# Ring tiles of split weights 64 bytes longer, and half the scratch for dynamic transfers

## The chip, the cores and the metric

The kernel runs on one NeuronCore of a Trainium2 chip. The metric is the device time of one execution in microseconds. A kernel is run several times and the median is taken; one more execution is recorded by the hardware profiler, and the profile and the trace are of that one.

The engines are named as in the profile: PE (matmuls), PEld (PE's weight loads, which overlap matmuls), DVE (VectorE), ACT (ScalarE), POOL (GpSimd), SP (SyncE, which issues most of the transfers).

## The reference

One layer of a hybrid encoder block in float32, 512 tokens by 1024 features: a norm, one input projection, three kinds of attention over its columns (4 + 6 + 6 heads), an output projection into the residual, a gated MLP with a causal convolution of width 3, and a gated embedding at the end.

```python
hn = rms_norm(h, ln_mix)
z = hn @ w_in                                  # 1024 x 3590, split into heads
o = concatenate([o_a, o_b, o_c])               # three kinds of softmax attention
h = h + o @ w_out                              # 1024 x 1024
u = rms_norm(h, ln_ffn) @ w_up                 # 1024 x 5632
c = conv_b + sum(conv_w[j] * shifted(u, 2 - j) for j in range(3))
h = h + (silu(c[:, :2816]) * c[:, 2816:]) @ w_down   # 2816 x 1024
gate = sigmoid(rms_norm(h, ln_ple) @ w_ple_gate)
h = h + (p @ w_ple_proj) * gate
```

## The kernel before

**Split operands.** Every float32 operand of a large matmul is split into a rounded part (float32r, "hi") and the rest ("lo"). ACT writes hi as a cast, DVE writes lo as raw - hi (in a few places POOL does, or an adding transfer). A product is then three matmuls, hi x hi, hi x lo and lo x hi, which `mm3` (line 223) issues into one PSUM bank. Its first operand is the stationary one (128 x 128), its second the moving one (up to 512 columns).

**Rings of weight tiles.** The pool `pi` (line 148) holds three rings: `wraw` with 4 tiles, `whi` and `wlo` with 8 each, all [128, 768] in 4-byte elements, that is 3072 bytes in each partition. Three places take tiles from them: `load_w` (line 151) for the input projection and the output projection, `first_products` (line 312) for the weights A0 of the first products, and `in_turn` (line 193) for the MLP and the gate, which keeps tiles and hands them out in turn: 7 of `whi`, 7 of `wlo`, and 6 raw ones, of which four are `wraw`, the fifth is the last of `whi` and the sixth the last of `wlo`. In the profile the ring tiles are named w_raw, w_hi, w_lo, and A_h, B_h, C_l, wo_h and so on.

**What is stationary.** In the input projection (`project`, line 442) a slice of Th or Tl, the split activations, is stationary, and 256 to 384 columns of a weight tile move (A_z, A0b_z, A1b_z, B_z, C_z). In the output projection (wo), the up projection (u, sX, sY, sZ), the down projection (dn_X, dn_Y, dn_Z) and the gate (pg, pp), a 128-column slice of a weight tile is stationary. What moves there is 512 columns of Th or Tl, or 256 columns of the tiles xh, xl, g_ah and g_al.

**Where the tiles lie.** The scratch of the transfers that POOL issues lies at byte 0 of each partition and is 16384 bytes long. Behind it come constants, then h, Th, Tl, some small tiles, and the rings. The pools of the attention (p1) and of the MLP (mp) are counted from the other end of the partition and share that room one after the other. In the program's memory map the places, as bytes modulo 512, are:

| tiles | place modulo 512 |
|---|---|
| h, Th, Tl, all tiles of the three rings | 128 |
| MLP: xh, xl, g_ah, g_al, c, hn, su, sm, pp (pool mp) | 128 |
| attention: oall, q, k, kl, bias | 192 |
| attention: V, zn, ptc | 352 |
| attention: pth, ptl, ot | 480 |

A slice of 128 elements is 512 bytes, so every slice of a ring tile lies at the same place as its tile. The rings end at byte 128640, and mp begins at that byte.

**Order of work.** The attention half (up to some 300 us) is ordered by the framework's scheduler, which simulates the engines from the instructions and their shapes. Behind it, a planner in the kernel (from line 1007) puts tasks in order by costs and due times that are written as functions of the element counts; DVE, ACT, POOL and SP then follow that order exactly. SP issues the loads of raw tiles; such a load waits until the split that read the tile before is done. POOL issues the adding transfers which form sums of weight blocks in DRAM (dsum, usum; `add_sums`, line 1168), one at a time. These go through queue 0, and so do the adding transfers of `load_w` (line 174).

Of the kernel before, what the change touches and what calls it, by code (L numbers as in the profile page):

```python
# [8 lines left out]
F32 = mybir.dt.float32  # L9
F32R = mybir.dt.float32r  # L10
# [5 lines left out]
P = 128  # L16
# [62 lines left out]
def kernel(ctx: ExitStack, tc: tile.TileContext, x, xt0, xt, pt_in, small, bias_c,  # L79
# [9 lines left out]
    nc = tc.nc  # L89
    def f32(ap):  # L90
        return ap.bitcast(F32)
# [52 lines left out]
    def col(c0, i=0):  # L144
        return cols[:, c0 + i : c0 + i + 1]


    pi = ctx.enter_context(tc.tile_pool(name="pi", bufs=1))
    W = {"pool": pi, "n": 768, "raw": 4, "hi": 8, "lo": 8}

    def load_w(src_fn, nk, m, n, name, eng=dve, gain=None, later=False):

        wp, we = W["pool"], W["n"]
        raw = wp.tile([P, we], F32, tag="wraw", bufs=W["raw"], name=f"{name}_r")
        for dst, src in src_fn(raw):
            dma = sp.dma_start(out=dst, in_=src)
            if later:
                tc.keep_in_program_order(dma)
        hi = wp.tile([P, we], F32R, tag="whi", bufs=W["hi"], name=f"{name}_h")
        lo = wp.tile([P, we], F32R, tag="wlo", bufs=W["lo"], name=f"{name}_l")  # L160
        hv, lv = (t[:, : nk * n].rearrange("p (k c) -> p k c", k=nk) for t in (hi, lo))
        rv = raw[:, : nk * m].rearrange("p (k c) -> p k c", k=nk)
        if later:
            def split():
                act.copy(hv[:, :, :m], rv)
                eng.tensor_tensor(out=lv[:, :, :m], in0=rv, in1=f32(hv[:, :, :m]), op=ALU.subtract)
                return hv, lv

            return split
        if eng == "dma":  # L170

            act.copy(hv[:, :, :m], rv)
            act.activation(lv[:, :, :m], rv, AF.Copy, scale=-1.0)
            nc.gpsimd.dma_start(out=lv[:, :, :m], in_=rv, accum_op=ALU.add)
            return hv, lv
        if gain is not None and eng is nc.gpsimd:
            for k in range(nk):
                eng.tensor_scalar(rv[:, k], rv[:, k], gain[:, k : k + 1], 1.0, ALU.mult, ALU.mult)
        if gain is None or eng is nc.gpsimd:
            act.copy(hv[:, :, :m], rv)  # L180
            eng.tensor_tensor(out=lv[:, :, :m], in0=rv, in1=f32(hv[:, :, :m]), op=ALU.subtract)
        else:
            for k in range(nk):
                hk, lk, rk = (v[:, k, :m] for v in (hv, lv, rv))
                act.activation(hk, rk, AF.Copy, scale=gain[:, k : k + 1])
                dve.scalar_tensor_tensor(lk, rk, gain[:, k : k + 1], f32(hk), ALU.mult, ALU.subtract)
        return hv, lv
# [5 lines left out]
    def in_turn(what, n):  # L193
        ring = RING[what]
        if len(ring) < n:
            tag = what
            if what == "raw" and len(ring) >= W["raw"]:
                tag = ("hi", "lo")[(len(ring) - W["raw"]) % 2]
            ring.append(pi.tile([P, 768], F32 if what == "raw" else F32R, tag=f"w{tag}", bufs=W[tag], name=f"w_{what}{len(ring)}"))
        else:  # L200
            ring.append(ring[-n])
        return ring[-1]

    def raw_tile():
        return in_turn("raw", NRAW)

    def split(t, n, gain=None, to=None, eng=dve):

        hi, lo = to or [in_turn(q, NHI)[:, :n] for q in ("hi", "lo")]
        if gain is None:  # L210
            act.copy(hi, t[:, :n])
            eng.tensor_tensor(out=lo, in0=t[:, :n], in1=f32(hi), op=ALU.subtract)
        else:
            act.activation(hi, t[:, :n], AF.Copy, scale=gain)
            dve.scalar_tensor_tensor(lo, t[:, :n], gain, f32(hi), ALU.mult, ALU.subtract)
        return hi, lo
# [21 lines left out]
    def tcol(T, k, t):  # L238
        return T[k // 4][:, k % 4, t * P : (t + 1) * P]
# [28 lines left out]
    def load_x(t):  # L268
        tc.keep_in_program_order(nc.sync.dma_start(out=h[:, t, :], in_=x[t * P : (t + 1) * P, :]))
# [36 lines left out]
    def stats(t):  # L306
        token_stats(t, h[:, t, :], ap.tile([P, D], BF16, tag="e3", bufs=2, name=f"n1_sq{t}"))
        done("n", t)
# [3 lines left out]
    def first_products():  # L312
        for k in range(KD):
            n = 384
            if k % 2 == 0:
                wh, wl = (pi.tile([P, 768], F32R, tag=f"w{q}", bufs=W[q], name=f"A0_{k // 2}_{q}") for q in ("hi", "lo"))
            a = slice((k % 2) * n, (k % 2 + 1) * n)
            th, tl = Th[k // 4][:, k % 4, :], Tl[k // 4][:, k % 4, :]
            g = h[:, 3, 0:1] if k == 0 else col(C_MIX, k)
            if k == 0:  # L320
                for c in (slice(0, H), slice(H, S)):
                    dve.tensor_scalar(th[:, c], XB[k][:, c], g, 1.0, ALU.mult, ALU.mult)
            elif k == 3:
                dve.tensor_scalar(th, XB[k], g, 1.0, ALU.mult, ALU.mult)
            else:
                act.activation(th, XB[k], AF.Copy, scale=g)
            act.copy(wh[:, a], WA[k])
            dve.tensor_tensor(out=wl[:, a], in0=WA[k], in1=f32(wh[:, a]), op=ALU.subtract)
            dve.scalar_tensor_tensor(tl, XB[k], g, f32(th), ALU.mult, ALU.subtract)
            for i, (ta, w) in enumerate(((Th, wh), (Th, wl), (Tl, wh))):  # L330
                for t in range(NT):
                    pe.matmul(z0[t][:, :n], tcol(ta, k, t), w[:, a], start=k == 0 and i == 0, stop=k == KD - 1 and i == 2)
            if k == 1:
                load_x(3)
        ws = [w() for w in first_b]
        for t in range(NT):
            stats(t)
        ev = [in_unit("A0", 0, 384, t, None, []) for t in range(NT)]

        rs = [ev[t][0](rest=False) for t in range(2)]  # L340
        for t in range(NT):
            ev[t][1](rs[t])
            if t < 2:
                rs.append(ev[t + 2][0](rest=False))
        for t in range(NT):
            ev[t][0](sums=False)
        return ws
# [105 lines left out]
    def in_unit(pr, part, n, t, ws, prefetch):  # L453

        name = f"{pr}{'b' if part else ''}"
        if t == 0:
            ZN[pr, part] = ap.tile([P, NT, 2 * P], F32, tag="zn", bufs=2, name=f"{name}_zn")
            if part == 0:
                V[pr] = ap.tile([P, NT, 2 * P], F32R, tag="V", bufs=3, name=f"{pr}_V")
        if pr == "A0" and part == 0:  # L460
            z = z0[t]
        else:
            z = bank("tots"[t] if pr == "A0" else "z", f"{name}_z{t}")

        def evac(sums=True, rest=True):
            if not rest:
                return qk_sums(z, t, name)
            if part == 0:
                v = V[pr]
                vh = bass.AP(v.tensor, v[:, t, :].offset, [v.ap[0], [192, 2], [1, HD]])  # L470
                zv = z[:, 2 * P : 3 * P].rearrange("p (g c) -> p g c", c=HD)
                act.activation(vh, zv, AF.Copy, scale=rstd[:, t, 2:3])
                dve.scalar_tensor_tensor(v[:, t, HD : HD + P].rearrange("p (g c) -> p g c", c=HD), zv,
                                               rstd[:, t, 2:3], f32(vh), ALU.mult, ALU.subtract)
            elif n > 2 * P:
                dve.scalar_tensor_tensor(fg[:, t, 0:6], z[:, 2 * P : 2 * P + 6], rstd[:, t, 2:3], fgb,
                                               ALU.mult, ALU.add)
            return qk_sums(z, t, name) if sums else None

        def evac_done(rs=None):  # L480
            qk_scale(z, ZN[pr, part], t, rs or evac())
            done("in", pr, part, t)

        if pr == "A0" and part == 0:
            return evac, evac_done
        return project(ws, n, t, z, evac_done, prefetch)
# [369 lines left out]
    for j, (pr, part, *_) in enumerate(PARTS[1:], 1):  # L856
        n = w_in[j].shape[3]
        nxt = []
        if j + 1 < len(PARTS):
            q = PARTS[j + 1]  # L860
# [109 lines left out]
    for f in SEVEN:  # L970
        w = bass.AP(cols.tensor, cols[:, C_CONV0 + NF + f : C_CONV0 + NF + f + 1].offset, [cols.ap[0], [2 * NF, 3]])
# [694 lines left out]
    while ready:  # L1666
        q = ready.pop()
# [27 lines left out]
    while order:  # L1695
# [3 lines left out]
        if now:  # L1699
            q = now[0]  # L1700
        else:
            tr = [(trial(q)[0], q) for q in can]
            first_at = max(min(x for x, _ in tr), clock["dve"])
            q = min((q for x, q in tr if x <= first_at + 0.1), key=lambda q: q.dl)

            late = min((q for x, q in tr if x <= first_at + SLACK), key=lambda q: q.dl)
            q = late if late.dl < q.dl - URGENT else q
# [74 lines left out]
```

## Time and profile before

| | us |
|---|---|
| median of 3 runs | 712.01 (711.25 to 712.97) |
| profiled execution, its time | 713.37 |
| profiled execution, span from the first to the last instruction | 711.5 |
| PE busy | 695.4 |
| DVE busy | 545.8 |
| ACT busy | 394.2 |
| POOL busy | 223.1 |

The rows of the profile that the prediction quotes are of these kinds. A row of the window view has the stretch, its length, the busy time and count of PE, PEld, DVE, ACT and POOL, the granted share of PE's clock, the busy share of the DMA engines and GB/s. A row of the waits has who waited for whom, total us, times, longest. A row of the timeline has start, length, engine, operation, tiles, shape and count. A row of the groups has line, engine, operation, output<-inputs (for matmuls: moving and stationary in no fixed order), shapes and count, then busy us, mean ns of one, and the idle time in front. All of them stand at line 105, which is the helper that issues each operation. Numbers in tile names are left out, so u stands for u0 to u43.

### The profile page before, as it was taken

To read this page: it belongs to the slowest core of one execution; us is meant where nothing else is said; L and a number is where in the kernel's file an instruction comes from. 1 tells how busy PE (TensorE), PEld (TensorE's weight loads), DVE (VectorE), ACT (ScalarE), POOL (GpSimd) and SP (SyncE) were. 2 spreads that over 40 slices of the span, in tenths; PEclk is the share of its full clock that TensorE was granted. 3 is DMA by queue.
4 is the path that set the end of the run, shared out by engine and by line. 5 is a ranking of instruction groups with operands and counts; after the bars stand their busy time and mean duration, and the time that the engine had idled before them with its cause. 6 is when DMAs were issued, how large, how long until landed. Compare 5 with 4: busy or idle time off the path is not lost.

```text
span 711.5 us, 11539 instructions
## 1 busy us (share of the span) xinstructions
PE 695.4 (98%) x4028; PEld 622.6 (88%) x4028; DVE 545.8 (77%) x1110; ACT 394.2 (55%) x737; POOL 223.1 (31%) x324
## 2 busy tenths in 40 slices
PE   9999999999999999999999999999999999999997
PEld 8988889988999988868888899988988888999786
DVE  7668887887878874788887884798776787788764
ACT  6746766766666762566454542554444555546831
POOL 4576776767665440420011110111101110001310
PEclk9999999999999999999999999999999999999999
DMA  9454669646335313452786888867986683652531
GB/s 329 174 150 101 195 178 241 210 158 197 105 122 179 126 42 115 142 195 95 171 178 136 244 194 187 194 165 197 230 206 141 145 210 82 216 164 82 177 111 67
DMA packets 48472, 116.52 MB, mean 164 GB/s; under 512 B 5495, under 2 KB 7159, under 8 KB 48413
## 3 DMA queue, kind: packets, MB, share of 16 engines
q1 hardware_dynamic: 40476, 96.59, 41.9%
q0 software_dynamic: 7648, 18.88, 16.7%
q8 instruction: 32, 0.52, 0.3%
q10 hardware_dynamic: 288, 0.30, 0.1%
q14 instruction: 28, 0.22, 0.1%
HBM read 108.53 MB, written 31.47 MB: 197 GB/s over the span
## 4 chain that ended last, share of the span: by engine, by line
PE 78%; DVE 7%; DMA 6%; ACT 4%; POOL 2%; issue 2%; SPq 0%; ACTq 0%; DVEq 0%; POOLq 0%
PE u L105 30%; PE dn_X L105 9%; PE C_z L105 6%; PE pg L105 6%; PE wo L105 5%; PE dn_Y L105 4%; PE B_z L105 4%; PE dn_Z L105 2%; DMA bias_B<-fk_d 1%; PE sX L105 1%; DMA h<-in_x_dram 1%; DMA waq<-in_w_in_dram 1%; PE C_s L105 1%; PE C_po L105 1%; PE A_z L105 1%
## 5 line engine op out<-in xcount | busy, mean ns | idle before, releaser
L105 PE MATMUL u<-Tl,w_hi 128*128 128x512 f32 x320 | 125.0, 391 | 0.5 <-DVE Tl L105 0.5
L105 PE MATMUL u<-Th,w_hi 128*128 128x512 f32 x320 | 124.8, 390 | 0.0
L105 PE MATMUL u<-Th,w_lo 128*128 128x512 f32 x320 | 124.6, 389 | 0.0
L105 ACT CAST w_hi<-w_raw 128x768 fp32r<-128x768 f32 (+1 forms) x116 | 88.2, 783 | 64.1 <-PE dn_X L105 21.1
L105 DVE TENSOR_TENSOR w_lo<-w_raw,w_hi 128x768 fp32r<-128x768 f32 (+1 forms) x114 | 101.5, 909 | 18.2 <-ACT w_hi L105 17.2
L105 DVE SCALAR_TENSOR_TENSOR c<-u,cols,c 128x511 f32<-128x511 f32 x80 | 59.5, 746 | 22.3 <-ACT c L105 21.3
L105 PEld LDWEIGHTS u<-Tl,w_hi 128*128 128x128 f32 x320 | 60.1, 188 | 13.5 <-DVE Tl L105 1.3
L105 PEld LDWEIGHTS u<-Th,w_hi 128*128 128x128 f32 x320 | 60.1, 188 | 12.6 <-ACT Th L105 0.5
L105 PEld LDWEIGHTS u<-Th,w_lo 128*128 128x128 f32 x320 | 60.1, 188 | 12.6 <-POOL w_lo L105 0.2
L105 ACT ACTIVATE c<-u,cols 128x512 f32<-128x512 f32 x40 | 31.1, 777 | 25.4 <-PE u L105 25.2
L105 PE MATMUL dn_X<-g_ah,w_lo 128*128 128x256 f32 x144 | 40.8, 283 | 0.0
L105 PE MATMUL dn_X<-g_al,w_hi 128*128 128x256 f32 x144 | 40.8, 283 | 0.0
L105 PE MATMUL dn_X<-g_ah,w_hi 128*128 128x256 f32 x144 | 40.7, 283 | 0.0
L105 POOL DMA_DIRECT2D dsum<-dsum x16 | 13.0, 812 | 85.8 <-DMA dsum<-dsum 62.1
L105 POOL DMA_DIRECT2D dsum<-in_w_dadd_dram x16 | 13.1, 821 | 85.0 <-DMA dsum<-in_w_dadd_dram 68.6
L105 PE MATMUL B_z<-B_h,Th 128*128 128x384 f32 x96 | 34.4, 358 | 0.8 <-DVE B_zn L105 0.6
L105 PE MATMUL C_z<-C_h,Th 128*128 128x384 f32 x96 | 34.3, 357 | 0.0
L105 PE MATMUL B_z<-B_h,Tl 128*128 128x384 f32 x96 | 32.4, 337 | 0.0
L105 PE MATMUL C_z<-C_h,Tl 128*128 128x384 f32 x96 | 32.3, 337 | 0.0
L105 PE MATMUL C_z<-C_l,Th 128*128 128x384 f32 x96 | 32.2, 336 | 0.0
L105 PE MATMUL B_z<-B_l,Th 128*128 128x384 f32 x96 | 32.2, 336 | 0.0
L105 DVE TENSOR_TENSOR h<-h,dn_X 128x512 f32<-128x512 f32 x24 | 16.4, 685 | 16.4 <-PE dn_X L105 16.4
(506 smaller groups left out, 2094.2 us busy)
## 6 DMA issues: line engine op xcount, KB each, us to landing
w_raw<-in_w_up_dram SPq DMA_DIRECT2D x44, 384.0 KB, 5.1
dsum<-in_w_dsum_dram SPq DMA_DIRECT2D x12, 768.0 KB, 6.6
w_raw<-dsum SPq DMA_DIRECT2D x24, 384.0 KB, 4.6
w_raw<-in_w_down_dram SPq DMA_DIRECT2D x18, 384.0 KB, 4.2
w_raw<-in_w_up_dram SPq DMA_DIRECT2D x20, 256.0 KB, 4.8
B_r<-in_w_in_dram SPq DMA_DIRECT2D x12, 384.0 KB, 3.7
C_r<-in_w_in_dram SPq DMA_DIRECT2D x12, 384.0 KB, 4.3
dsum<-in_w_dadd_dram POOLq DMA_DIRECT2D x12, 384.0 KB, 6.6
```

The costliest lines, as they stand in the source:

```text
L105: ins = getattr(self.eng, op)(*a, **k)
```

## The change

Tiles of the rings `whi` and `wlo` become [128, 784] instead of [128, 768]: 3136 bytes, which is 6 x 512 + 64. The 16 elements at the end of each are never written or read. Tile i of a ring then lies at (128 + 64 i) modulo 512, so the eight tiles of a ring lie at eight different places. The `wraw` tiles stay as they are; the fifth and sixth raw tile, which come from the other two rings, are longer too. The 16 longer tiles take 1024 bytes more of each partition. The scratch for POOL's transfers is set to 8192 bytes instead of the default 16384, which moves h, Th, Tl and the raw ring down by 8192 bytes, 16 x 512, so their places modulo 512 stay at 128. The pools at the other end stay where they are.

```diff
     pi = ctx.enter_context(tc.tile_pool(name="pi", bufs=1))
+    STEP = 16
     W = {"pool": pi, "n": 768, "raw": 4, "hi": 8, "lo": 8}
...
-        hi = wp.tile([P, we], F32R, tag="whi", bufs=W["hi"], name=f"{name}_h")
-        lo = wp.tile([P, we], F32R, tag="wlo", bufs=W["lo"], name=f"{name}_l")
+        hi = wp.tile([P, we + STEP], F32R, tag="whi", bufs=W["hi"], name=f"{name}_h")
+        lo = wp.tile([P, we + STEP], F32R, tag="wlo", bufs=W["lo"], name=f"{name}_l")
...
-            ring.append(pi.tile([P, 768], F32 if what == "raw" else F32R, tag=f"w{tag}", bufs=W[tag], name=f"w_{what}{len(ring)}"))
+            ring.append(pi.tile([P, 768 if tag == "raw" else 768 + STEP], F32 if what == "raw" else F32R, tag=f"w{tag}", bufs=W[tag], name=f"w_{what}{len(ring)}"))
...
-                wh, wl = (pi.tile([P, 768], F32R, tag=f"w{q}", bufs=W[q], name=f"A0_{k // 2}_{q}") for q in ("hi", "lo"))
+                wh, wl = (pi.tile([P, 768 + STEP], F32R, tag=f"w{q}", bufs=W[q], name=f"A0_{k // 2}_{q}") for q in ("hi", "lo"))
...
-    nc = _bacc.Bacc("TRN2", target_bir_lowering=False, num_devices=1)
+    nc = _bacc.Bacc("TRN2", target_bir_lowering=False, num_devices=1, dynamic_dma_scratch_size=8192)
```

## The prediction

> **What bounds the kernel now.** I read the page first (busy time, the slices), then the busy time of one long window, PE's waits in it, and last the groups of matmuls by shape.
>
> ```profile
> span 711.5 us, 11539 instructions
> PE 695.4 (98%) x4028; PEld 622.6 (88%) x4028; DVE 545.8 (77%) x1110; ACT 394.2 (55%) x737; POOL 223.1 (31%) x324
> PE   9999999999999999999999999999999999999997
> PEclk9999999999999999999999999999999999999999
> 300.00:711.50 411.50, 405.19 (x2313) 356.14 (x2311) 315.01 (x462) 204.88 (x303) 49.03 (x57) 1.00 0.64 165
> PE pst L105 <- DVE sums L105: 0.7, 1, 0.7
> PE u L105 <- DVE Tl L105: 0.5, 2, 0.2
> PE pg L105 <- DVE Tl L105: 0.4, 1, 0.4
> ```
>
> PE is busy in every slice and the clock is whole. From 300 us to the end PE works 405.2 of 411.5 us, while DVE is busy for 315 and ACT for 205. The three rows under that are all of PE's waits in this stretch: 1.6 us. So a faster or slower split, or an earlier or later load, has next to nothing to give there. The time of this stretch is the number of matmuls times the distance from one start to the next, and the timeline shows that distance:
>
> ```profile
> 428.05 0.28 PE L105 MATMUL dn_X<-g_ah,w_hi 128*128 128x256 f32 x1
> ...
> 429.25 0.28 PE L105 MATMUL dn_X<-g_al,w_hi 128*128 128x256 f32 x1
> 430.88 0.39 PE L105 MATMUL u<-Th,w_hi 128*128 128x512 f32 x1
> ...
> 432.24 0.39 PE L105 MATMUL u<-Th,w_hi 128*128 128x512 f32 x1
> ```
>
> Ten matmuls of 256 columns in 1.20 us are 120 ns each; six of 512 columns in 1.36 us are 227 ns each. The difference, 107 ns for 256 columns, is 2.4 columns per ns; what is left, 13 ns, does not grow with the columns. A matmul's listed duration runs past its successor's start by a constant 163 ns (283 against 120, 389 or 390 against 227, in the groups below), so mean durations of groups can be compared in place of distances.
>
> **The change part by part.** It adds and removes no instruction, no element and no wait; the two orders (the scheduler's in the attention, the planner's behind it) know shapes and not addresses, so I take every queue's order as unchanged. Three things move.
>
> *The splits.* ACT's cast and DVE's subtraction write and read the same 768 elements at other addresses. The question is whether an address has a price on these engines, and the trace of before has operands at unlike places: oall lies at 192 modulo 512 and Th at 128, the pth and ptl tiles at 480, g_al, c and g_ah all at 128.
>
> ```profile
> L105 DVE TENSOR_TENSOR w_lo<-w_raw,w_hi 128x768 fp32r<-128x768 f32 x88 | 82.9, 953 | 18.2 <-ACT w_hi L105 17.2
> L105 DVE TENSOR_TENSOR g_al<-c,g_ah 128x512 fp32r<-128x512 f32 x9 | 6.2, 684 | 0.0
> L105 DVE TENSOR_TENSOR Tl<-oall,Th 128x512 fp32r<-128x512 f32 x7 | 4.8, 687 | 1.2 <-ACT Th L105 1.2
> L105 DVE TENSOR_TENSOR C_ptl<-C_pt,C_pth 128x512 fp32r<-128x512 f32 x6 | 4.1, 689 | 1.0 <-ACT C_pth L105 1.0
> ```
>
> 684 with equal places, 687 and 689 with unlike ones: 0.7% at most. On 88 long subtractions that is 88 x 7 ns = 0.6 us of DVE time, and DVE has 96 us to spare behind 300 us. I cost it at 0; without the cover it would be those 0.6 us, and 0 to 0.6 go into the range.
>
> *The matmuls.* A ring tile is the stationary operand of the MLP, of the output projection and of the gate, and the moving operand of the input projection. Today each of its 128-column slices starts at 128 modulo 512, as do Th, Tl, g_ah, g_al, xh and xl: stationary and moving always start at the same place. After the change one ring tile in eight still does; for 7/8 of these matmuls the two start 64 to 448 bytes apart. No matmul with a ring weight shows that now, so its price has to come from the nearest rows. The product of probabilities and values has it: V at 352 is stationary, pth and ptl at 480 move. Beside them stand the score matmuls, where q, k and kl all lie at 192, and the weight matmuls at 128.
>
> ```profile
> L105 PE MATMUL u<-Th,w_hi 128*128 128x512 f32 x320 | 124.8, 390 | 0.0
> L105 PE MATMUL u<-Th,w_lo 128*128 128x512 f32 x320 | 124.6, 389 | 0.0
> L105 PE MATMUL wo<-Th,wo_l 128*128 128x512 f32 x64 | 25.0, 391 | 0.0
> L105 PE MATMUL C_s<-kl,C_q_q 128*128 128x512 f32 x6 | 2.4, 392 | 0.0
> L105 PE MATMUL B_s<-kl,B_q_q 128*128 128x512 f32 x6 | 2.3, 391 | 0.0
> L105 PE MATMUL A_po<-A_ptl,A_V 128*128 128x512 f32 x4 | 1.6, 392 | 0.0
> L105 PE MATMUL B_po<-B_pth,B_V 128*128 128x512 f32 x6 | 2.4, 397 | 0.0
> L105 PE MATMUL C_po<-C_pth,C_V 128*128 128x512 f32 x6 | 2.4, 394 | 0.0
> L105 PE MATMUL C_po<-C_ptl,C_V 128*128 128x512 f32 x6 | 2.4, 396 | 0.0
> L105 PE MATMUL C_s<-kl,C_q_q 128*128 128x384 f32 x6 | 2.0, 339 | 0.0
> L105 PE MATMUL C_po<-C_pth,C_V 128*128 128x384 f32 x6 | 2.0, 338 | 0.0
> L105 PE MATMUL C_z<-C_l,Th 128*128 128x384 f32 x96 | 32.2, 336 | 0.0
> ```
>
> With 512 columns the unlike places stand at 392, 397, 394 and 396, mean 394.8; the equal ones at 389 to 392, mean 390.6. That is 4.2 ns more. With 384 columns it is 338 against 339 in the same stage and 336 in C_z: between -1 and +2, I take +0.5. The sample is small (22 matmuls against hundreds) and all of it lies in the attention, where PE changes from one kind of work to another, so the low end is 0 (the two kl rows are within 2 ns of A_po). The high end is 8 ns, the best equal row against the worst unlike one (397 - 389).
>
> How many matmuls pay it: each row below is one of three groups of its kind.
>
> ```profile
> L105 PE MATMUL pg<-Th,w_lo 128*128 128x512 f32 x28 | 10.9, 390 | 0.0
> L105 PE MATMUL pp<-pT_al,w_hi 128*128 128x512 f32 x16 | 6.2, 389 | 0.0
> L105 PE MATMUL B_z<-B_l,Th 128*128 128x384 f32 x96 | 32.2, 336 | 0.0
> L105 PE MATMUL A_z<-A_h,Tl 128*128 128x384 f32 x32 | 11.2, 351 | 0.0
> L105 PE MATMUL A_z<-A_lo,Th 128*128 128x384 f32 x32 | 6.9, 338 | 0.0
> ```
>
> 512 columns: 3 x (320 + 64 + 28 + 16) = 1284, of which 7/8 are 1124; at 4.2 ns 4.7 us. 384 columns: 3 x (96 + 96 + 32 + 32) = 768, 7/8 are 672; at 0.5 ns 0.3 us, and they lie in the attention, where part of PE's time is waiting, so I count 0.
>
> With 256 columns the trace has no row at all with unlike places. Rows at equal places differ among themselves:
>
> ```profile
> L105 PE MATMUL dn_X<-g_ah,w_lo 128*128 128x256 f32 x144 | 40.8, 283 | 0.0
> L105 PE MATMUL dn_Y<-g_ah,w_lo 128*128 128x256 f32 x72 | 20.4, 283 | 0.0
> L105 PE MATMUL dn_Z<-g_ah,w_lo 128*128 128x256 f32 x36 | 10.2, 283 | 0.0
> L105 PE MATMUL C_po<-ptc,C_V 128*128 128x256 f32 x24 | 3.8, 280 | 0.0
> L105 PE MATMUL A_0b_s<-kl,A_q_q 128*128 128x256 f32 x4 | 1.1, 278 | 0.0
> ```
>
> 283 in a long run, 278 to 280 where PE changes work (ptc and V both lie at 352). The bounds are -5 ns (what a 256-wide matmul can lose) and +4 ns (as for 512); I take 0, since the spread is there without a difference of place. On 3 x (144 + 72 + 36) = 756, 7/8 of them 662, that is -3.3 to +2.6 us for the range.
>
> *The scratch.* It serves the transfers that POOL issues (queue 0).
>
> ```profile
> q0 software_dynamic: 7648, 18.88, 16.7%
> L105 POOL DMA_DIRECT2D dsum<-in_w_dadd_dram x16 | 13.1, 821 | 85.0 <-DMA dsum<-in_w_dadd_dram 68.6 <-DMA usum<-usum 9.6 <-DMA dsum<-dsum 6.8
> ```
>
> 7648 packets on 16 engines are 478 for each over the whole kernel, and the adding transfers go one at a time: POOL idles for 85 us before 16 issues of 0.82 us, mostly until the transfer before has landed. [...] Cost 0. [...]
>
> **Sum.** 4.7 + 0 + 0 + 0 = 4.7 us. The profiled execution has a span of 711.5 and took 713.4, so some 1.9 lie around the span; it would come to 718.1. The median of the runs, 712.0, is 1.4 below that execution; from it the forecast is 716.7, and I write 716.5, because the attention hides a little of the 192 matmuls of wo.
>
> **The rivals.**
>
> *No place has a price: 712.0.* For it: the 384-wide rows, the DVE rows, and A_po at 392, a hair from kl. Against it: three of the four 512-wide rows. [...]
>
> *Faster: the 13 ns are the price of equal places.* PE loads the next weights while a matmul runs (PEld is busy for 622.6 us beside PE's 695.4), step after step in the same rhythm, so two streams that begin at one place could meet in one fixed way, each time. The place is PE's reading of SBUF, the price 5 ns (283 to 278) for each matmul that begins elsewhere: 662 of 256 columns alone, 3.3 us, or with the 1124 of 512 columns 8.9 us; between them 706.0. It decides as soon as dn_X stands at 280 or less. Against it: the unlike 512-wide rows lie above the equal ones, and not one below 389.
>
> *A chain on POOL becomes late.* If less scratch made each of the adding transfers (two kinds of 16 for the down projection) wait one issue more, 32 x 0.82 = 26 us would be added to a chain whose ends PE waits for; at most that, and 718.6 if slack takes three quarters. Nothing in the trace speaks for it but POOL's idle time.
>
> **How the numbers follow.** A price at 512 columns 0.42, no price 0.26, faster 0.27, POOL 0.03, and 0.02 for a slower turn of another kind. About 0.2%, 1.4 us, is what a measurement of this kernel can tell from no change. The case of no price gives all its weight to the same; the forecast's lower end (1 ns, 1.1 us) gives 0.02 to it. Faster 0.27, same 0.28, slower 0.45. The forecast's own range is 713.4 to 721 (1 to 8 ns at 1124 matmuls). The whole range, 706 to 720, leaves out half of the faster case's lower tail and the highest prices, under 0.2 together.
>
> **What would show it.** Right: u and wo at 393 to 396 and dn_X still at 283, DVE's w_lo at 953, the waits of PE behind 300 us unchanged. u at 389 to 391 with the same total speaks for no price; dn_X at 280 or under for the faster rival; a PE wait on a w_hi or w_lo that came from dsum or usum for the POOL rival. The forecast is wrong as a whole if the order of an engine's instructions changes, since then the difference may have nothing to do with places.

## The result and the profile after

| | before | after |
|---|---|---|
| median of 13 runs each, us | 712.01 | 714.39 |
| ratio after / before | | 1.0028, 95% interval 1.0016 to 1.0040 |
| profiled execution, its time, us | 713.37 | 713.58 |
| its span, us | 711.5 | 711.8 |

The kernel became slower by 0.28% of 712.0, some 2.0 us (0.16 to 0.40%, 1.1 to 2.8 us; the two medians are 2.4 us apart). The forecast was 4.5 us over the median of before. Every engine has the same instructions in the same order as before.

The page of after, its first lines and the granted clock:

```profile
span 711.8 us, 11539 instructions
PE 695.5 (98%) x4028; PEld 618.8 (87%) x4028; DVE 547.0 (77%) x1110; ACT 394.4 (55%) x737; POOL 223.0 (31%) x324
PEclk9999999999999999999999999999999999999999
```

The window of after from 300 us to the end (its columns as in the prediction's row of before), and PE's waits in it:

```profile
300.00:711.80 411.80, 405.37 (x2310) 352.96 (x2308) 314.76 (x460) 204.35 (x302) 49.09 (x57) 1.00 0.64 164
PE pg L105 <- DVE Tl L105: 0.8, 1, 0.8
PE pst L105 <- DVE sums L105: 0.5, 1, 0.5
PE u L105 <- DVE Tl L105: 0.4, 2, 0.2
```

PE still bounds the kernel, at the full clock, and waits for 1.7 us where it waited for 1.6. Nothing became late. What moved is inside the matmuls. Two groups of before that are not shown above, then the groups of after by shape:

```profile
L105 PE MATMUL dn_X<-g_ah,w_hi 128*128 128x256 f32 x144 | 40.7, 283 | 0.0
L105 PE MATMUL sX<-xl,w_hi 128*128 128x256 f32 x16 | 4.5, 283 | 0.0
```

```profile
L105 PE MATMUL u<-Th,w_hi 128*128 128x512 f32 x320 | 126.2, 394 | 0.0
L105 PE MATMUL wo<-Th,wo_l 128*128 128x512 f32 x64 | 25.2, 394 | 0.0
L105 PE MATMUL pp<-pT_al,w_hi 128*128 128x512 f32 x16 | 6.3, 393 | 0.0
L105 PE MATMUL dn_X<-g_ah,w_hi 128*128 128x256 f32 x144 | 40.3, 280 | 0.0
L105 PE MATMUL sX<-xl,w_hi 128*128 128x256 f32 x16 | 4.5, 281 | 0.0
L105 DVE TENSOR_TENSOR w_lo<-w_raw,w_hi 128x768 fp32r<-128x768 f32 x88 | 83.0, 954 | 18.8 <-ACT w_hi L105 18.0
```

Matmuls of 512 columns became longer (u 390 to 394, wo 391 to 394, pp 389 to 393), those of 256 columns shorter (dn_X 283 to 280, sX 283 to 281). The subtraction is where it was, 954 against 953.

The two spans differ by only 0.3 us although the runs differ by 2.0. The reason is read from the first start of the output projection, in the view of one tile (count, ns minimum/median/maximum, first and last start). First before, then after:

```profile
L105 PE MATMUL wo<-Th,wo_h x64: 388/389/482, 241.7 to 297.4; 128*128 128x512 f32 x64
```

```profile
L105 PE MATMUL wo<-Th,wo_h x64: 387/397/483, 240.3 to 296.7; 128*128 128x512 f32 x64
```

The attention, in front of wo, ended 1.4 us earlier in the profiled execution of after. Over all profiled executions of this study wo starts between 238.4 and 242.5 us, with no order by kernel. From wo's first start to the end of the span, however, PE hardly waits (2.0 us before, 2.1 after): 711.5 - 241.7 = 469.8 us before and 711.8 - 240.3 = 471.5 after, 1.7 us more. I call this the **PE stretch**; it is the measure in the table of the experiments. It comes from one profiled execution of each kernel, but it tells kernels apart to a few tenths: before and the three kernels below that restore its rows stand at 469.8 or 469.9.

Where the 1.7 us come from follows from the start-to-start distances of all matmuls of these two widths in the PE stretch, less the streaming time (columns divided by 2.4 per ns, the rate between before's medians, 120 ns at 256 columns and 227 at 512); some 25 distances that exceed it by more than 40 ns, around waits and changes of work, are left out:

| | before, ns above streaming | after | number | difference, us |
|---|---|---|---|---|
| 512 columns | 13.7 | 17.1 | 1360 | +4.6 |
| 256 columns | 13.2 | 10.7 | 1162 | -2.9 |

4.6 - 2.9 = 1.7. After's distances differ with the place of the stationary tile less that of the moving one. The places are from the program's memory map, and the stationary tile counted here is that of the next matmul, whose load the trace shows beside the present one (in before, the load for the u matmul of 429.49 us starts at 429.37, with the last dn_X matmul of its run). With 512 columns the median is 13.7 ns at 0 and at 256 bytes, 19.7 at 64 and at 320, 17 to 18 at 128, 192, 384 and 448. With 256 columns it is 13.3 at 0 and at 256 bytes, 6.3 at 64, and 10 to 13 at the others.

### The profile page after: what moved, and what is told of

It reads as the page before. It is cut to its first block, busy times and chain, and to the rows that moved or that the text cites. A ratio compares the mean times of both kernels' runs of the same rounds, so it can differ in the third digit from the quotient of the medians.

```text
span 711.8 us, 11539 instructions
## 1 busy us (share of the span) xinstructions
PE 695.5 (98%) x4028; PEld 618.8 (87%) x4028; DVE 547.0 (77%) x1110; ACT 394.4 (55%) x737; POOL 223.0 (31%) x324
## 4 chain that ended last, share of the span: by engine, by line
PE 78%; DVE 8%; DMA 4%; ACT 4%; POOL 2%; issue 2%; SPq 0%; DVEq 0%; POOLq 0%; ACTq 0%
PE u L105 30%; PE dn_X L105 9%; PE C_z L105 7%; PE pg L105 6%; PE wo L105 5%; PE dn_Y L105 4%; PE B_z L105 4%; PE dn_Z L105 2%; DMA bias_B<-fk_d 2%; PE sX L105 1%; DMA h<-in_x_dram 1%; PE C_s L105 1%; PE C_po L105 1%; PE B_s L105 1%; DVE A_e L105 1%
## 5 line engine op out<-in xcount | busy, mean ns | idle before, releaser
L105 PEld LDWEIGHTS u<-Tl,w_hi 128*128 128x128 f32 x320 | 60.2, 188 | 14.4 <-DVE Tl L105 1.3
```

Of the source, the lines that this page charges most:

```text
L105: ins = getattr(self.eng, op)(*a, **k)
```

## The experiments

Theory: a matmul's distance to the next depends on the place of the weight against that of the moving tile modulo 512 bytes, upward for 512 columns and downward for 256, and the change is the sum of both. Rivals: the longer tiles or the smaller scratch do it; the tiles of a ring must differ among themselves; the absolute place counts. All kernels but the first two are made from before. The scratch had to be set to 15,360 or 15,872 bytes in them to make room for a longer tile; the first two experiments show what that is worth. "PE stretch" is the span less wo's first start. The places are those of the large groups. A few small ones lie otherwise: pp (48 matmuls) has its moving tile in mp, the sums that read Th or Tl (72 of 256 columns) go with Th, and part of pg (72 and 48) has a weight wg of its own, which lies in mp.

| kernel | place of weight less moving tile, bytes: 512 columns / 256 columns | u, ns | dn_X, ns | PE stretch, us | ratio to before |
|---|---|---|---|---|---|
| before | 0 / 0 | 390 | 283 | 469.8 | |
| after | eight places / eight places | 394 | 280 | 471.5 | 1.0028 [1.0016, 1.0040] |
| e1_long512 | 0 / 0 | 390 | 283 | 469.9 | 1.0011 [0.9996, 1.0026] |
| e2_scratch15k | eight / eight | 394 | 280 | 471.5 | 1.0024 [1.0011, 1.0037] |
| e3_ring64 | 64 / 64 | 395 | 276 | 470.6 | 1.0018 [0.9999, 1.0036] |
| e4_mlp64 | 0 / 64 | 389 | 280 | 467.1 | 0.9949 [0.9933, 0.9965] |
| e5_th_ring192 | 0 / 64 | 390 | 281 | 467.2 | 0.9936 [0.9914, 0.9957] |
| e6_ring256 | 256 / 256 | 390 | 283 | 469.8 | 0.9989 [0.9974, 1.0003] |
| e7_all192 | 0 / 0, all 64 further | 390 | 283 | 469.9 | 0.9992 [0.9978, 1.0007] |
| e8_ring32 | 32 / 32 | 396 | 281 | 475.2 | 715.36 us, one run |
| e9_ring_mp192 | 64 / 0 | 395 | 283 | 476.6 | 1.0105 [1.0083, 1.0126] |
| e10_th_ring224 | 0 / 96 | 390 | 281 | 469.3 | 0.9998 [0.9985, 1.0011] |

**Longer tiles without other places** (e1_long512), made from after:

```diff
-    STEP = 16
+    STEP = 128
```

> The ring tiles are 512 bytes longer instead of 64, so all of them lie at 128 modulo 512 again; the scratch is 8192 bytes as in the changed kernel. Theory (the time goes by where the stationary tile lies against the moving one, modulo 512): all groups as before the change, u at 389 to 391 ns, dn_X at 283, ratio 1.000 to the kernel before. Rival (the halved scratch, or tiles that lie elsewhere and are longer, cost the time): ratio 1.003 with dn_X at 283.

The groups of e1_long512 by shape:

```profile
L105 PE MATMUL u<-Th,w_hi 128*128 128x512 f32 x320 | 124.8, 390 | 0.0
L105 PE MATMUL dn_X<-g_ah,w_hi 128*128 128x256 f32 x144 | 40.7, 283 | 0.0
```

With 512 bytes more for each tile, and the scratch of after, the rows of before are back, and the PE stretch with them.

**Other places with the scratch nearly whole** (e2_scratch15k), made from after:

```diff
-    nc = _bacc.Bacc("TRN2", target_bir_lowering=False, num_devices=1, dynamic_dma_scratch_size=8192)
+    nc = _bacc.Bacc("TRN2", target_bir_lowering=False, num_devices=1, dynamic_dma_scratch_size=15360)
```

> The eight places of the change, with a scratch of 15360 bytes instead of 8192. Theory (places): u at 393 to 394, dn_X at 280, ratio 1.003 as the changed kernel. Rival (scratch): ratio 1.000, since the scratch is almost what it was.

u 394, dn_X 280 and a PE stretch of 471.5, as after. The two together leave the places as the cause, and neither the tiles' length nor the scratch.

**One place for all ring tiles, 64 bytes off** (e3_ring64): the tile gq, which lies ahead of the rings, becomes 64 bytes longer.

```diff
-    gq = cp.tile([P, 8], F32, tag="gq", name="gq")
+    gq = cp.tile([P, 24], F32, tag="gq", name="gq")
```

> Tiles as before the change, but all three rings begin 64 bytes later, at 192 modulo 512, while Th, Tl, xh, xl, g_ah and g_al stay at 128. Theory (places; in the changed kernel tiles with this distance of 64 bytes stood 6 ns above the old spacing with 512 columns and 7 ns below it with 256): u at 395 to 396 ns, dn_X at 276, which is +8.2 us on 1368 matmuls of 512 columns and -6.7 us on 1139 of 256 columns, so ratio 1.002. Rival (what costs is that the tiles of a ring lie at unlike places among themselves, not against the moving tiles): u at 390, dn_X at 283, ratio 1.000.

The groups of e3_ring64 by shape:

```profile
L105 PE MATMUL u<-Th,w_hi 128*128 128x512 f32 x320 | 126.4, 395 | 0.0
L105 PE MATMUL dn_X<-g_ah,w_hi 128*128 128x256 f32 x144 | 39.8, 276 | 0.0
L105 PE MATMUL sX<-xl,w_hi 128*128 128x256 f32 x16 | 4.4, 276 | 0.0
```

Here the ring tiles do not differ among themselves, and both effects are there, larger than in after: the distances are 5.6 ns longer at 512 columns (19.3 against 13.7) and 6.1 ns shorter at 256 (7.1 against 13.2). On 1361 and 1162 matmuls that is +7.6 and -7.1 us, which nearly cancel (PE stretch +0.8). So it is the weight against the moving tile that counts. The total alone, 1.0018, would have hidden both terms.

**The gain alone, in two ways.** In e4_mlp64 the last tile of the pool mp, which fills from the other end, becomes 64 bytes longer, so xh, xl, g_ah, g_al and the others of mp lie at 64, and Th and the rings stay at 128:

```diff
-                pin = mp.tile([P, D + 88], F32, tag="pin", bufs=1, name="sums3")
+                pin = mp.tile([P, D + 104], F32, tag="pin", bufs=1, name="sums3")
```

> Rings as before the change, at 128 modulo 512; the tiles of the MLP pool (xh, xl, g_ah, g_al, c and so on) begin 64 bytes earlier, at 64. The stationary weights then lie 64 bytes behind the moving tiles for the 256-wide matmuls of the down projection and of the sums, while Th and Tl stay at 128 with the rings for the 512-wide ones. Theory (places): dn_X at 276, u at 390, some 6.7 us less, ratio 0.9905. Rival (a 256-wide matmul gained in the changed kernel because the ring tiles lie apart from one another): dn_X at 283, ratio 1.000.

In e5_th_ring192 an unused tile of 64 bytes stands ahead of Th, so Th, Tl and the rings lie at 192 and mp stays at 128:

```diff
+    cp.tile([P, 16], F32, tag="pad64", name="pad64")
     Th = [cp.tile([P, 4, S], F32R, tag=f"Th{g}", name=f"Th{g}") for g in range(2)]
```

> The kernel before, with an unused tile of 64 bytes between the residual and the two halves of the transposed activations (Th, Tl): Th, Tl and the three rings then lie at 192 modulo 512, the moving tiles of the MLP stay at 128. Matmuls of 512 columns then have weight and activations at equal places (but pp, whose moving tile is an MLP tile), those of 256 columns read a weight 64 bytes beyond. Theory (place of weight against activations, as the ring at 192 showed it for both widths): u and wo stay at 389 to 391 ns, dn_X falls from 283 to 276, sX<-Th and the rest at equal places stay at 283; 7 ns on some 1000 matmuls of 256 columns is 7 us less, 705 us, ratio 0.990. Rival (the gain needs the 512-column matmuls to be slow as well, or the memory to be read at some absolute place): dn_X 280 or more, ratio 0.996 or above.

The groups of e4_mlp64, then of e5_th_ring192, by shape:

```profile
L105 PE MATMUL u<-Th,w_hi 128*128 128x512 f32 x320 | 124.6, 389 | 0.0
L105 PE MATMUL dn_X<-g_ah,w_hi 128*128 128x256 f32 x144 | 40.3, 280 | 0.0
```

```profile
L105 PE MATMUL u<-Th,w_hi 128*128 128x512 f32 x320 | 124.7, 390 | 0.0
L105 PE MATMUL pp<-pT_al,w_hi 128*128 128x512 f32 x16 | 6.3, 395 | 0.0
L105 PE MATMUL dn_X<-g_ah,w_hi 128*128 128x256 f32 x144 | 40.4, 281 | 0.0
```

Both kernels beat before and after: 708.49 and 708.66 us, where before ran at 712.29 and 711.89 beside them. u is as before, since Th and the weights are at equal places again; pp, whose moving tile is in mp, pays (395). Much of the gain that I had expected is missing, though. Some 7 us were expected of each; the ratios give 3.6 and 4.6 us and the PE stretches 2.7 and 2.6 (why these two measures differ is open), and dn_X is at 280 and 281 and not at 276. That 280 or more was the mark of the rival written down for e5_th_ring192, by which the gain needs slow matmuls of 512 columns as well; the rival's ratio, 0.996 or above, did not come, so it was half right. The timeline of e5_th_ring192 shows what is missing. The first two rows bound a run of dn matmuls between matmuls of u; the last two lie in a run behind sX<-Th, whose weight and moving tile are at one place:

```profile
413.64 0.28 PE L105 MATMUL dn_X<-g_ah,w_hi 128*128 128x256 f32 x1
...
422.12 0.39 PE L105 MATMUL u<-Th,w_hi 128*128 128x512 f32 x1
...
438.01 0.28 PE L105 MATMUL sX<-xh,w_hi 128*128 128x256 f32 x1
...
439.03 0.28 PE L105 MATMUL sX<-xh,w_hi 128*128 128x256 f32 x1
```

From 413.64 to 422.12 there are 72 matmuls at 117.8 ns each, 11.1 above streaming (8.48 us / 72); from 438.01 to 439.03 nine at 113.3 ns, 6.7 above it. Places and shapes are the same. A run of equal matmuls settles into one of two rhythms, and in this kernel 168 of 1020 distances at 64 bytes belong to the faster (under 9 ns above streaming). They all stand in the two stretches that come behind sums from Th, whose weight and moving tile are at equal places with 256 columns (51 of 54 distances and 117 of 120). In the nine stretches that come behind matmuls of 512 columns at equal places, none of the 846 is fast. In e3_ring64, where the runs of dn come behind slow matmuls of 512 columns, practically all are (1080 of 1092). So in these kernels the rhythm goes with what ran just before; no run changes that alone, and why it is so stays open.

**The period and the absolute place.** e6_ring256 has gq longer by 256 bytes, so the rings lie at 384:

```diff
-    gq = cp.tile([P, 8], F32, tag="gq", name="gq")
+    gq = cp.tile([P, 72], F32, tag="gq", name="gq")
```

> The kernel before, with the tile ahead of the rings longer, so that all three rings lie at 384 and everything else at 128: the distance is 256 bytes. Theory (the price has a period of 256 bytes, as after's rows at distances of 0 and 256 agree): u 389 to 391, dn_X 283, as before, ratio 1.000. Rival (any unlike place has a price): u 393 or more, dn_X 280 or less, ratio 1.002 as with the ring at 192.

e7_all192 is e5_th_ring192 with mp at 192 too:

```diff
-                pin = mp.tile([P, D + 88], F32, tag="pin", bufs=1, name="sums3")
+                pin = mp.tile([P, D + 200], F32, tag="pin", bufs=1, name="sums3")
```

> As the first of this set, but the MLP's moving tiles are at 192 as well: weights and activations lie at equal places again, all of them 64 bytes further than before. If only the difference of the places counts: u 389 to 391, dn_X 283, sX<-xl 283, ratio 1.000. If the absolute place counts too (the MLP tiles moved to 64 gave dn_X 280 where the rings moved to 192 gave 276, both at a distance of 64 bytes): dn_X off 283 by 2 ns or more, and the ratio off 1.000 by 0.003 or more, of either sign.

The groups of e6_ring256, then of e7_all192:

```profile
L105 PE MATMUL u<-Th,w_hi 128*128 128x512 f32 x320 | 124.9, 390 | 0.0
L105 PE MATMUL dn_X<-g_ah,w_hi 128*128 128x256 f32 x144 | 40.8, 283 | 0.0
```

```profile
L105 PE MATMUL u<-Th,w_hi 128*128 128x512 f32 x320 | 124.9, 390 | 0.0
L105 PE MATMUL dn_X<-g_ah,w_hi 128*128 128x256 f32 x144 | 40.8, 283 | 0.0
```

Both are before again, in rows, PE stretch (469.8 and 469.9 against 469.8) and ratio. A distance of 256 bytes is here as good as none, and moving everything together by 64 does nothing. A period of 256 bytes is not shown for every distance: after's medians at 64 and 320 bytes agree with 512 columns (19.7 both), but not with 256 (6.3 and 10.3, in a kernel where the two rhythms may mix). The reading by which the absolute place counts, which I had formed when e4_mlp64 and e3_ring64 differed, falls by e5_th_ring192 above all: its rings and mp lie where those of e3_ring64 do (192 and 128), and still dn_X is at 281 against 276, while e4_mlp64, with other places (128 and 64), agrees with it (280, PE stretch 467.1 against 467.2).

**Finer places.** e8_ring32 has gq of 16 elements (rings at 160), e10_th_ring224 has a tile of 24 elements in place of the 16 of e5_th_ring192 (Th and rings at 224).

> The kernel before with the three rings at 160, 32 bytes from everything else. If the price goes in steps of 64 bytes: u 390, dn_X 283, as before. If it goes by finer places: u above 391 and dn_X below 281, between the rows of before and those of the ring at 192 (395 and 276).

> As the kernel with Th, Tl and the rings at 192, but at 224: 96 bytes from the MLP's moving tiles instead of 64; 512 columns at equal places again (u 389 to 391). If any distance gives 256 columns the same gain: dn_X 280 or 281, ratio 0.994. If it depends on the distance (after's rows were 6.3, 13.3 and 10.3 ns above streaming at 64, 128 and 192 bytes): dn_X between 277 and 283, ratio 0.990 to 1.000.

32 bytes are enough for the price at 512 columns: u 396, 5.5 ns more distance, and the PE stretch is 5.4 us longer; the price does not go in steps of 64 bytes. At 256 columns 32 bytes gain 1.5 ns (11.7 against 13.2). The row of e10_th_ring224:

```profile
L105 PE MATMUL dn_X<-g_ah,w_hi 128*128 128x256 f32 x144 | 40.4, 281 | 0.0
```

At 96 bytes the 256-column distance is 12.1, a gain of 1.1 ns, although dn_X's mean duration is 281 as in e5_th_ring192, where the distance is 10.6. On 1162 matmuls 1.1 ns are 1.3 us, but the PE stretch is only 0.5 us shorter and the ratio 0.9998: the matmuls of 512 columns average 14.4 ns above streaming here against 13.7 before (1.0 us), mostly because pp and part of pg lie at unlike places there (pg's rows with wg stand at 392 to 399 ns, against 389 before). Between kernels that differ by a nanosecond or two, the mean duration of a group is too coarse, and so is the constant 163 ns by which the prediction took durations for distances; the distance of starts decides.

**The price alone** (e9_ring_mp192): gq as in e3_ring64 and the last tile of mp as in e7_all192, so rings and mp lie at 192 and Th at 128.

> The kernel before with the rings and the MLP's moving tiles at 192, Th and Tl left at 128: the complement of the kernel with Th, Tl and rings at 192. Only the matmuls of 512 columns on Th and Tl read an unlike place (64 bytes), those of 256 columns on xh, xl, ah and al an equal one. If the two widths are independent, u and wo rise to 395 or 396 and dn_X stays at 283; some 1240 matmuls of 512 columns by 6.3 ns (19.7 less 13.4 ns above the streaming time, as with the ring alone at 192) are 7.8 us: 719.7 us, ratio 1.011. Rival (the spacing of 256 columns follows from the state that the slow matmuls of 512 columns leave behind, and not from its own places): dn_X 280 or less and ratio 1.006 or below.

Its groups, and wo in the view of one tile:

```profile
L105 PE MATMUL u<-Th,w_hi 128*128 128x512 f32 x320 | 126.4, 395 | 0.0
L105 PE MATMUL pp<-pT_al,w_hi 128*128 128x512 f32 x16 | 6.2, 389 | 0.0
L105 PE MATMUL dn_X<-g_ah,w_hi 128*128 128x256 f32 x144 | 40.7, 283 | 0.0
```

```profile
L105 PE MATMUL wo<-Th,wo_h x64: 388/398/483, 239.2 to 295.9; 128*128 128x512 f32 x64
```

u pays, pp (equal places) does not, and dn_X stays at 283. 718.83 us beside 711.42: 1.0105 where 1.011 was expected. So the price at 512 columns stands by itself, and slow matmuls of 512 columns alone give no gain at 256. The gain needs its own unlike places; its size is not independent, since it is larger where the 512 columns are slow (distance 7.1 in e3_ring64, 10.6 in e5_th_ring192). In the PE stretch the price alone is +6.8 us and the gain alone -2.6 (e5_th_ring192); e3_ring64 has both, with 4.1 us more gain from the faster rhythm ((10.6 - 7.1) ns on 1162 matmuls). The sum is 6.8 - 2.6 - 4.1 = 0.1 us, and 0.8 was measured. The other 0.7 us are about what PE's waits differ by. From 300 us on they come to 2.0 us in e3_ring64, 1.1 here, 1.7 in e5_th_ring192 and 1.6 before, so 0.4 + 0.5 - 0.1 = 0.8. The wait that moves most, in e3_ring64 and then here:

```profile
PE pg L105 <- DVE Tl L105: 1.2, 1, 1.2
```

```profile
PE pg L105 <- DVE Tl L105: 0.3, 1, 0.3
```

## Why the prediction was wrong

- **Order, waits, splits, scratch, 384 columns: right.** The order is unchanged, PE's waits are 1.7 against 1.6 us, w_lo is at 954 and was to stay at 953, and e1_long512 and e2_scratch15k show the scratch to be worth nothing: with 8192 bytes and the places of before the PE stretch is 469.9 as against 469.8, with 15,360 bytes and the places of after 471.5 as against 471.5. How much of the scratch is in use at any moment no run shows; these two stretches are what stands for the 0 there. The 0 at 384 columns held too: those matmuls of the input projection stand 14.8 ns above streaming in both traces.
- **The term at 512 columns: right, in mechanism and size.** 4.7 us were forecast, from 4.2 ns (four rows of probabilities times values, against rows at equal places) on 1124 matmuls. The trace has 4.6 us. u, wo and pp at 393 to 394 lie where the forecast had them, 393 to 396. It is an average over places at which the price is 0 to 6 ns. By the memory map of after, 24 of the 1284 matmuls lie at 0 bytes (all of them wo, since the MLP and the gate keep seven tiles of each ring and leave the one at 128 to the raw weights) and 210 at 256, which pays nothing. So 1050 pay, at 4.3 ns on average (4.5 us). That the average comes so near to the 4.2 ns of rows at a single distance is partly luck. wo was thought to be hidden a little by the attention; its 192 matmuls take 56.85 us from first to last start and took 56.21, 0.64 us more, so it was not hidden. The range's lower end does not follow from its own term: 1 ns on 1124 matmuls is 1.1 us, which gives 713.1 and not 713.4.
- **The term at 256 columns: this is the step that failed.** The prediction took 0, "since the spread is there without a difference of place". It measured -2.9 us: -2.5 ns on 1162 matmuls, of which 1092 have a ring weight. The bounds of that step, -5 to +4 ns, held the value, and the lower of the rows it showed (ptc, 280, and A_0b_s, 278) lay nearer to what came; a spread among rows at equal places was no reason to expect 0 at unlike ones. The count was short as well: 756 dn matmuls on g_ah and g_al were counted, and 168 dn matmuls on xh and xl and 168 for sums (sX, sY, sZ) were left out. With both terms the sum is 4.6 - 2.9 = 1.7 us, and the runs gave 2.0.
- **The rival "faster" had half of the mechanism.** Its mark, dn_X at 280 or under, came true. It then gave the same sign to both widths or counted 256 columns alone; the width of 512 goes the other way. Its price of 5 ns at 256 columns was too high for after's mixed places (2.5) and too low for the best (6.1 in e3_ring64). Its 3.3 us for 256 columns alone are near the 2.9 measured by luck, since the price was twice too high and the count, 662 against 1092, too small.
- **The rival "no place has a price" fell.** e7_all192 and e9_ring_mp192 differ in where Th, Tl and some small constants lie, by 64 bytes, and by 6.7 us of PE stretch (469.9 against 476.6). u stands at 390 ns in the first and at 395 in the second, so a matmul's distance is not free of its addresses.
- **The POOL rival fell** with PE's waits, 1.7 us against 1.6.

Why the two widths go opposite ways is not shown. One row speaks to it, the weight load that runs beside a matmul. In before, then in e3_ring64:

```profile
L105 PEld LDWEIGHTS u<-Th,w_hi 128*128 128x128 f32 x320 | 60.1, 188 | 12.6 <-ACT Th L105 0.5
L105 PEld LDWEIGHTS dn_X<-g_ah,w_hi 128*128 128x128 f32 x144 | 27.6, 192 | 0.2
```

```profile
L105 PEld LDWEIGHTS u<-Th,w_hi 128*128 128x128 f32 x320 | 60.0, 188 | 14.5 <-ACT Th L105 0.2
L105 PEld LDWEIGHTS dn_X<-g_ah,w_hi 128*128 128x128 f32 x144 | 27.0, 188 | 0.3
```

With equal places the load beside 256 columns takes 192 ns, with unlike ones 188, as beside 512 columns in both. In front of these 144 loads beside 256 columns PEld is idle for 0.2 us in all, so the loads follow each other nearly without pause; in front of the 320 beside 512 columns it is idle for 12.6. Beside 256 columns the load thus becomes shorter together with the distance (13.2 to 7.1 ns above streaming), while beside 512 columns it stays at 188 ns and the distance grows (13.7 to 19.3). That narrow matmuls go at the pace of the loads and wide ones do not is a guess of mine from these rows, which no run tests, and the fit is loose: in e10_th_ring224 dn_X's loads take 188 to 189 ns too, with a distance of 12.1 ns above streaming.

## What to carry to other kernels

In this kernel, with PE busy for 98% of the span, the place of a weight tile against the moving tile is a parameter of its own: 64 bytes, for one width of matmul at a time, were worth between -0.6% (e5_th_ring192) and +1.1% (e9_ring_mp192) with not one instruction changed. In a kernel like this one (fp32r, a new 128 x 128 weight for each matmul), try wide matmuls (512 columns) at equal places or 256 bytes apart (u at 390 ns in both, 395 at 64 bytes) and narrow ones (256 columns) 64 bytes apart (dn_X at 276 to 281 ns, against 283), and read the result from start-to-start distances by width, since a small total can be two large terms that cancel. When a bound is open to both signs and its count is not small, "0" is a choice as strong as any other.

## What was not expected of the hardware

- The distance from one matmul to the next in fp32r is the streaming time and 13.2 to 13.7 ns at equal places (before); at 64 bytes the addition is 19.3 to 19.6 ns for 512 columns (e3_ring64, e9_ring_mp192) and 7.1 (e3_ring64) or 10.6 (e4_mlp64, e5_th_ring192) for 256. In these kernels it goes with the difference of the places: u and dn_X stand at 390 and 283 ns, as before, with 256 bytes between them (e6_ring256) and with all of them 64 bytes further (e7_all192), and 32 bytes already matter (512 columns: 19.2, e8_ring32).
- At 64 bytes a run of equal matmuls of 256 columns has two steady rhythms, 113 and 118 ns, and keeps one of them through the run: 120 matmuls in the faster and 420 in the slower are the longest of e5_th_ring192.
